# Encoder block on one core: the down projection's block outputs summed in DRAM by adding DMAs, its activation forms shared by both column halves, and 32 instead of 20 tiles of gate and up as block products

## The chip, the cores and the metric

The kernel runs on one core of a Trainium2 chip. The metric is the device time of one execution in microseconds (us), the median of several. The engines are named as in the profile: PE (TensorE, matrix products; PEld is its weight load), DVE (VectorE), ACT (ScalarE), POOL (GpSimd) and SP (SyncE, which here only issues DMAs).

## The reference, cut to what matters

```python
def reference(x, norm_mix, w_in, w_fourier, sgu_norm, w_spatial, b_spatial, w_out,
              norm_ffn, w_gate, w_up, w_down, norm_final):
    ...  # token mixing (Fourier heads and spatial gating) and the output projection, added to x
        h2 = rmsnorm(x, norm_ffn[l])
        x = x + (jax.nn.silu(h2 @ w_gate[l]) * (h2 @ w_up[l])) @ w_down[l]
    return rmsnorm(x, norm_final)
```

There are 512 tokens, the model width is 2048, the width of the feed-forward part 5632, all in float32. Only the feed-forward part (gate, up, down) and its sum into x are touched here.

## The kernel before, in words

Every float32 product is made of three products of rounded halves: an operand is split into `hi` (a cast on ACT, L173) and `lo` (the rest, a subtraction on DVE, L174), and PE computes hi·hi, hi·lo and lo·hi (L85 to L87, L705 to L707, L791 to L793).

The feed-forward part has 44 tiles of 128 features (FT). They are worked in three ways, in this order.

*Direct units.* A `GateUp` item is a quarter of the work of a tile: eight of the sixteen slices of the model width, for gate or for up. It loads 512 KB of weights, splits them, and runs 24 matmuls with 512 moving columns. Two units make gate, two make up. The first 4 tiles are worked so, and the last 20.

*Block products for gate and up.* Tiles 4 to 23 are worked in pairs. Gate (or up) of a pair is a 2x2 block product, done with seven products in place of eight in a Winograd-like scheme (`Matrix`, `Block`). Each of the seven takes 24 matmuls with 256 moving columns; the forms of h2 are prepared once (`Forms`).

*Block products for the down projection* (`Product`). The activations of the first 40 tiles go to a DRAM buffer `ad` and come back as `ac`. For each of ten groups q of four tiles and each half np_ of the output columns, seven products are made, 140 in all. A product takes 12 matmuls with 512 columns. On DVE it needs: `sums` (sums of weight blocks of 128x1024, and of activation blocks of 128x512: the form x), `prep` (the split of the form X, 128x512, and of the weights, 128x1024), and `out`, which adds the product from PSUM into output blocks that stay in SBUF. Before, these are eight blocks `x` of 128x1024 (they start as the x of the residual, read from the DRAM buffer `xd` by `Outputs`) and two common sums `u`; `Fold` adds u to the blocks after the last product. Then come four `Last` items and the tail with the last four tiles, the final norm and the store.

`drive` writes the order of PE, DVE, ACT, POOL and SP by hand. At item k it records the sums of item k+3, the split of item k+2, the loads of items k+4 to k+8, then the matmuls and the `out` of item k. So DVE, which works in order, stands at the `out` of item k until PE has ended it, with items k+1 and k+2 split. The list `items` sets how products are mixed with direct units: `LAG` units come first, and then products are spread evenly over the units that follow. All 512 KB buffers of this part share a pool of 26 slots (`spool`).

Of the kernel before, what the change touches and what calls it, by code (L numbers as in the profile page):

```python
# [10 lines left out]
F32 = mybir.dt.float32  # L11
# [25 lines left out]
FIRST, BLOCKS = 4, 20  # L37
# [3 lines left out]
def encoder_block(ctx, tc, a, out):  # L41
# [21 lines left out]
    def slot(name, dtype=F32, shape=(P, U)):  # L63
        return spool.tile(list(shape), dtype, tag="s", name=name)
# [374 lines left out]
    xd = dram.tile([NT, 2, P, U], F32, name="xd")  # L439
# [170 lines left out]

    GORDER = (1, 6, 2, 7, 5, 4, 3)
# [109 lines left out]

    PRODUCTS = {}

    class Product(Item):
# [19 lines left out]
        def sums(self):  # L744
            i, r = self.i, PRODUCTS[self.q, self.np_]
            A11, A12, A21, A22 = self.blocks()
            add, sub = nc.vector.tensor_add, nc.vector.tensor_sub
            if i == 1:
                add(r[12], r[12], r[22])
            elif i == 6:  # L750
                x = slot(f"x{self.name}", F32, (P, 2, 2, H))
                r["x5"], r["x6"] = x[:, 0], x[:, 1]
                sub(r["x5"], A21, A22)
                sub(r["x6"], r["x5"], A11)
                add(r[11], r[11], r[12])
            elif i == 5:
                add(r[21], r[21], r[11])
                sub(r[11], r[11], r[22])
            elif i == 7:
                sub(r["x5"], A11, A21)  # L760
            elif i == 3:
                add(r["x6"], r["x6"], A12)

        def behind(self, y):
            same = isinstance(y, Product) and (y.q, y.np_) == (self.q, self.np_)
            return same and (y.i, self.i) in ((1, 6), (2, 5), (5, 7))

        def prep(self):
            i, r = self.i, PRODUCTS[self.q, self.np_]
            A11, A12, A21, A22 = self.blocks()  # L770
            x = {1: A11, 2: A12, 4: A22, 5: r.get("x5"), 7: r.get("x5")}.get(i, r.get("x6"))
            self.X = slot(f"X{self.name}", F32R, (P, 2, 2, H))
            split(x, (self.X[:, 0], self.X[:, 1]))
            raw = r[{1: 11, 6: 11, 2: 21, 7: 12, 5: 11, 4: 21, 3: 22}[i]]
            self.split_weights(raw, f"d{self.name}")
# [31 lines left out]
    class Fold(Item):


        def __init__(self, np_):  # L810
            self.np_ = np_

        def out(self):
            for t in range(2):
                for k in (12, 21, 22):
                    d = out_block(k, t, self.np_)
                    nc.vector.tensor_tensor(d, d, usum[self.np_][:, t, :], op=ALU.add if k == 21 else ALU.subtract)
# [75 lines left out]
    items += [Fold(0), Fold(1), Split(1)]  # L893
# [3 lines left out]
    works = [x for x in items if not isinstance(x, (Split, Fold, Forms, Outputs))]  # L897
# [159 lines left out]
```

## Time and profile before

| | |
|---|---|
| time, median of 3 runs | 1861.09 us (1860.4 to 1861.54) |
| profiled execution | 1861.64 us, span 1859.9 us |
| granted TensorE clock, mean | 0.995 of full speed |
| PE, DVE, ACT, POOL busy | 1837.2, 1432.5, 738.7, 84.4 us |
| tiles 4 to 23 as block products | about 574 to 981 us |
| direct units mixed with down products | 981 to 1798 us |

The shares are averages over stages; what limits a stage is read from its own window.

### The profile page before, as it was taken

How to read it: one execution, taken by the hardware profiler on the slowest of the kernel's cores; microseconds unless marked ns; L12 is line 12 of the kernel's file. 1: busy time of each engine (PE TensorE's matmuls, PEld its weight loads, DVE VectorE, ACT ScalarE, POOL GpSimd, SP SyncE). 2: the span in 40 equal slices, each digit the busy share in tenths (PEclk: the TensorE clock that was granted, in tenths of full speed). 3: DMA queues.
4: the chain of work that ended last, by engine and by line, in shares of the span. 5: the costliest groups of instructions: out<-in, count | busy, mean ns of one | idle time of the engine just before them, and what ended most of it. 6: DMA issues, size and time to landing. Idle time of an engine off the chain costs nothing.

```text
span 1859.9 us, 24373 instructions
## 1 busy us (share of the span) xinstructions
PE 1837.2 (99%) x9810; PEld 1592.8 (86%) x9810; DVE 1432.5 (77%) x1805; ACT 738.7 (40%) x950; POOL 84.4 (5%) x82
## 2 busy tenths in 40 slices
PE   9999999999999999999999999999999999999996
PEld 7888888888888999999998888888888888888875
DVE  7554654333578888888887899999899889889987
ACT  6345532222333434444443433334333434334334
POOL 5001110000000000000000000000000000000004
PEclk9999999999999999999999999999999999999998
DMA  7322224442441433433328323333232433323223
GB/s 243 98 76 95 91 80 145 138 136 91 134 172 69 135 127 104 134 115 103 111 72 294 136 91 124 131 141 136 91 136 91 165 118 116 122 102 117 98 79 126
DMA packets 65201, 227.12 MB, mean 122 GB/s; under 512 B 7616, under 2 KB 7744, under 8 KB 65088
## 3 DMA queue, kind: packets, MB, share of 16 engines
q1 hardware_dynamic: 60768, 209.83, 32.8%
q0 software_dynamic: 4320, 15.73, 2.2%
q8 instruction: 77, 1.26, 0.3%
q14 instruction: 36, 0.29, 0.1%
HBM read 206.66 MB, written 18.87 MB: 121 GB/s over the span
## 4 chain that ended last, share of the span: by engine, by line
PE 95%; DVE 2%; ACT 1%; issue 0%; DMA 0%; POOL 0%; SPq 0%; ACTq 0%; DVEq 0%
PE d L793 7%; PE d L792 7%; PE d L791 7%; PE g L86 5%; PE g L87 5%; PE g L85 5%; PE up L86 4%; PE up L87 4%; PE up L85 4%; PE upb L707 4%; PE upb L706 4%; PE upb L705 4%; PE gb L707 4%; PE gb L705 4%; PE gb L706 4%; PE o L87 3%
## 5 line engine op out<-in xcount | busy, mean ns | idle before, releaser
L791 PE MATMUL d<-hi_d,X 128*128 128x512 f32 x560 | 217.8, 389 | 0.0
L792 PE MATMUL d<-lo_d,X 128*128 128x512 f32 x560 | 217.8, 389 | 0.0
L793 PE MATMUL d<-hi_d,X 128*128 128x512 f32 x560 | 217.8, 389 | 0.0
L173 ACT CAST hi_d<-w 128x1024 fp32r<-128x1024 f32 x140 | 147.5, 1053 | 153.9 <-PE d L793 54.5
L174 DVE TENSOR_TENSOR lo_d<-w,hi_d 128x1024 fp32r<-128x1024 f32 x140 | 170.4, 1217 | 5.2 <-ACT hi_d L173 5.2
L85 PE MATMUL up<-h2hi,hi_up 128*128 128x512 f32 x384 | 149.5, 389 | 0.0
L85 PE MATMUL g<-h2hi,hi_g 128*128 128x512 f32 x384 | 149.5, 389 | 0.0
L86 PE MATMUL up<-h2lo,hi_up 128*128 128x512 f32 x384 | 149.4, 389 | 0.0
L86 PE MATMUL g<-h2lo,hi_g 128*128 128x512 f32 x384 | 149.4, 389 | 0.0
L87 PE MATMUL g<-h2hi,lo_g 128*128 128x512 f32 x384 | 149.4, 389 | 0.0
L87 PE MATMUL up<-h2hi,lo_up 128*128 128x512 f32 x384 | 149.4, 389 | 0.0
L802 DVE TENSOR_TENSOR x<-d,x 128x512 f32<-128x512 f32 x200 | 130.4, 682 | 0.0
L792 PEld LDWEIGHTS d<-lo_d,X 128*128 128x128 f32 x560 | 105.1, 188 | 21.8
L791 PEld LDWEIGHTS d<-hi_d,X 128*128 128x128 f32 x560 | 105.1, 188 | 21.8
L793 PEld LDWEIGHTS d<-hi_d,X 128*128 128x128 f32 x560 | 105.1, 188 | 21.7
L80 DVE TENSOR_TENSOR lo_o<-raw_o,hi_o 128x1024 fp32r<-128x1024 f32 x32 | 39.2, 1225 | 102.4 <-ACT hi_o L79 102.4
L173 ACT CAST hi_gb<-w_gb 128x1024 fp32r<-128x1024 f32 x70 | 73.4, 1049 | 92.8 <-DVE w_gb L640 26.6
L173 ACT CAST hi_upb<-w_upb 128x1024 fp32r<-128x1024 f32 x70 | 73.5, 1049 | 84.7 <-PE upb L706 29.2
L174 DVE TENSOR_TENSOR lo_upb<-w_upb,hi_upb 128x1024 fp32r<-128x1024 f32 x70 | 85.4, 1221 | 23.5 <-ACT hi_upb L173 23.5
L174 DVE TENSOR_TENSOR lo_gb<-w_gb,hi_gb 128x1024 fp32r<-128x1024 f32 x70 | 85.5, 1221 | 22.1 <-ACT hi_gb L173 22.1
L173 ACT CAST hi_g<-raw_g 128x1024 fp32r<-128x1024 f32 x48 | 50.3, 1054 | 111.5 <-PE up L86 35.3
L706 PE MATMUL gb<-hf,hi_gb 128*128 128x256 f32 x320 | 90.7, 283 | 0.4 <-DVE hf L174 0.4
(319 smaller groups left out, 4835.3 us busy)
## 6 DMA issues: line engine op xcount, KB each, us to landing
w<-in_w_down SPq DMA_DIRECT2D x80, 512.0 KB, 6.0
raw_g<-in_w_gate SPq DMA_DIRECT2D x48, 512.0 KB, 3.6
raw_up<-in_w_up SPq DMA_DIRECT2D x48, 512.0 KB, 3.5
w_gb<-in_w_gate SPq DMA_DIRECT2D x40, 512.0 KB, 4.2
w_upb<-in_w_up SPq DMA_DIRECT2D x40, 512.0 KB, 4.4
raw_o<-in_w_out SPq DMA_DIRECT2D x32, 512.0 KB, 3.5
ac<-ad SPq DMA_DIRECT2D x20, 512.0 KB, 5.2
raw_v<-in_w_v SPq DMA_DIRECT2D x16, 512.0 KB, 3.5
```

Source lines behind the costliest of these rows:

```text
L85: mm(ps, lhs[0], rhs[0], start=first, stop=False)
L86: mm(ps, lhs[0], rhs[1], start=False, stop=False)
L87: mm(ps, lhs[1], rhs[0], start=False, stop=last)
L173: nc.scalar.copy(dst[0], src)
L174: nc.vector.tensor_sub(dst[1], src, dst[0])
L705: mm(ps, lhs[0], rhs[0], start=first, stop=False, skip_group_check=True)
L706: mm(ps, lhs[0], rhs[1], start=False, stop=False, skip_group_check=True)
L707: mm(ps, lhs[1], rhs[0], start=False, stop=last, skip_group_check=True)
L791: mm(p, X[:, 0, j, l], hi, start=j == 0 and not more, stop=False, skip_group_check=True)
L792: mm(p, X[:, 0, j, l], lo, start=False, stop=False, skip_group_check=True)
L793: mm(p, X[:, 1, j, l], hi, start=False, stop=j == 1, skip_group_check=True)
L802: nc.vector.tensor_add(d, self.ps[t], d)
```

## The change

Gate and up: `BLOCKS` grows from 20 to 32, so tiles 4 to 35 are block products, and 8 tiles (32 units) are left as direct units after them instead of 20 (80 units). Down: the residual is written to a DRAM buffer `cd` in the shape of the eight output blocks. The running sums of a 7-product set now live in two buffers `u` and `w`; the four output blocks of a set are written to a buffer `c` and added to `cd` by a DMA of POOL with `accum_op=add`. `Outputs` reads `cd` back once, after the products; `Fold` is gone. The forms x and their splits X are made for np_ 0 alone and kept for np_ 1. The order of the seven becomes 1, 6, 2, 7, 5, 4, 3. The products are spread over the units 1 to 26 of 32 (`LAG, END = 1, 5`) instead of 3 to 78 of 80.

```diff
-FIRST, BLOCKS = 4, 20
+FIRST, BLOCKS = 4, 32
...
-                nc.gpsimd.dma_start(xd[m, n // 2], x2[m][n // 2])
+                to = cd[n // 2, m // 2, :, :, m % 2, :].rearrange("c p s -> p c s")
+                nc.gpsimd.dma_start(to, x2[m][n // 2].rearrange("p (c s) -> p c s", s=S))
...
-    ORDER = (1, 6, 2, 5, 7, 3, 4)
+    ORDER = (1, 6, 2, 7, 5, 4, 3)
...
-                usum[np_] = slot(f"u{np_}", F32, (P, 2, S))
-                nc.gpsimd.memset(usum[np_], 0.0)
-                for k in (11, 22, 12, 21):
+                for k in (11, 12, 21, 22):
                     t = cs_[k, np_] = slot(f"x{k}_{np_}", F32, (P, 2, S))
+                    nc.sync.dma_start(t, cd[np_, k // 10 - 1, k % 10 - 1])
...
         def sums(self):
+            if self.np_ == 0:
+                A11, A12, A21, A22 = self.blocks()
+                if i == 6:
+                    x = slot(f"x{self.name}", F32, (P, 2, 2, H))
+                    r["x5"], r["x6"] = x[:, 0], x[:, 1]
+                    sub(r["x5"], A21, A22)
+                    sub(r["x6"], r["x5"], A11)
+                elif i == 7:
+                    r["x7"] = slot(f"x{self.name}", F32, (P, 2, H))
+                    sub(r["x7"], A11, A21)
+                elif i == 3:
+                    add(r["x6"], r["x6"], A12)
...
         def prep(self):
+            if self.np_ == 0:
...
+                X = XS[self.q, i] = slot(f"X{self.name}", F32R, (P, 2, 2, H))
+                split(x, (X[:, 0], X[:, 1]))
+            self.X = XS[self.q, i]
...
         def out(self):
-                nc.vector.tensor_add(d, self.ps[t], d)
-                if i == 7:
-                    d = out_block(22, t, np_)
-                    nc.vector.tensor_sub(d, d, self.ps[t])
-    class Fold(Item):
...
+                if i == 1:
+                    nc.scalar.copy(u, ps)
+                elif i == 6:
+                    nc.vector.tensor_add(u, ps, u)
+                elif i == 2:
+                    nc.scalar.copy(c[:, t, :], ps)
+                elif i == 7:
+                    nc.vector.tensor_add(w, ps, u)
+                elif i == 5:
+                    nc.vector.tensor_sub(c[:, t, :], ps, w)
+                elif i == 4:
+                    nc.vector.tensor_add(c[:, t, :], ps, w)
                 else:
+                    nc.vector.tensor_sub(c[:, t, :], ps, u)
+            if to:
+                nc.gpsimd.dma_start(cd[self.np_, to // 10 - 1, to % 10 - 1], c, accum_op=ALU.add)
...
-    LAG = 3
+    LAG, END = 1, 5
...
-        want = min(len(products), len(products) * max(0, n + 1 - LAG) // (len(units) - LAG - 1))
+        want = min(len(products), len(products) * max(0, n + 1 - LAG) // (len(units) - LAG - END))
...
+        if n == len(units) - END + 1:
+            items.append(Outputs())
```

On DVE, in a set of the second column half (np_ 1), from the split of product 2 on. Names read tile, q, np_, product; `raw_g` and `act` belong to direct units. Before:

```order
L174 TENSOR_TENSOR X0_1_2_9294<-ac1_8673,X0_1_2_9294 128x512
L174 TENSOR_TENSOR lo_d0_1_2_9298<-w21_0_1_9080,hi_d0_1_2_9297 128x1024
L757 TENSOR_TENSOR w21_0_1_9080<-w21_0_1_9080,w11_0_1_9053 128x1024
L758 TENSOR_TENSOR w11_0_1_9053<-w11_0_1_9053,w22_0_1_9057 128x1024
L802 TENSOR_TENSOR u1_8850<-d0_1_6_0_9303,u1_8850 128x512
L802 TENSOR_TENSOR u1_8850<-d0_1_6_1_9304,u1_8850 128x512
L174 TENSOR_TENSOR X0_1_5_9319<-x0_1_6_9218,X0_1_5_9319 128x512
L174 TENSOR_TENSOR lo_d0_1_5_9323<-w11_0_1_9053,hi_d0_1_5_9322 128x1024
L760 TENSOR_TENSOR x0_1_6_9218<-ac0_8671 128x512
L174 TENSOR_TENSOR lo_g26_1_9355<-raw_g26_1_9195,hi_g26_1_9354 128x1024
L802 TENSOR_TENSOR x11_1_8852<-d0_1_1_0_9278,x11_1_8852 128x512
L802 TENSOR_TENSOR x11_1_8852<-d0_1_1_1_9279,x11_1_8852 128x512
```

Now, in the same half of another group:

```order
L174 TENSOR_TENSOR lo_d4_1_2_13520<-w21_4_1_13352,hi_d4_1_2_13519 128x1024
L756 TENSOR_TENSOR w21_4_1_13352<-w21_4_1_13352,w11_4_1_13296 128x1024
L554 TENSOR_TENSOR act19_12907<-g39_13377,rstdB_101 128x512
L758 TENSOR_TENSOR w11_4_1_13296<-w11_4_1_13296,w22_4_1_13300 128x1024
L174 TENSOR_TENSOR lo_d4_1_7_13563<-w12_4_1_13298,hi_d4_1_7_13562 128x1024
L566 SCALAR_TENSOR_TENSOR act19_12907<-s39_13558,act19_12907 128x512
L806 TENSOR_TENSOR uw4_1_1_13516<-d4_1_6_0_13569,uw4_1_1_13516 128x512
L806 TENSOR_TENSOR uw4_1_1_13516<-d4_1_6_1_13570,uw4_1_1_13516 128x512
L174 TENSOR_TENSOR lo_d4_1_5_13586<-w11_4_1_13296,hi_d4_1_5_13585 128x1024
L174 TENSOR_TENSOR lo_d4_1_4_13606<-w21_4_1_13352,hi_d4_1_4_13605 128x1024
```

The splits X, the form x and the outputs of products 1 and 2 are gone from DVE in this half. In the first half (np_ 0) the splits and forms stay, as here between the products 3 and 2 of two sets:

```order
L174 TENSOR_TENSOR X4_0_1_13237<-ac8_13091,X4_0_1_13237 128x512
L174 TENSOR_TENSOR lo_d4_0_1_13241<-w11_4_0_13095,hi_d4_0_1_13240 128x1024
L744 TENSOR_TENSOR x4_0_6_13244<-ac8_13091,ac9_13093 128x512
L745 TENSOR_TENSOR x4_0_6_13244<-x4_0_6_13244,ac8_13091 128x512
L754 TENSOR_TENSOR w11_4_0_13095<-w11_4_0_13095,w12_4_0_13097 128x1024
L814 TENSOR_TENSOR c3_1_4_13262<-d3_1_4_0_13248,uw3_1_7_13181 128x512
L814 TENSOR_TENSOR c3_1_4_13262<-d3_1_4_1_13249,uw3_1_7_13181 128x512
L174 TENSOR_TENSOR X4_0_6_13266<-x4_0_6_13244,X4_0_6_13266 128x512
L174 TENSOR_TENSOR lo_d4_0_6_13270<-w11_4_0_13095,hi_d4_0_6_13269 128x1024
L816 TENSOR_TENSOR c3_1_3_13285<-d3_1_5_0_13219,uw3_1_1_13115 128x512
L816 TENSOR_TENSOR c3_1_3_13285<-d3_1_5_1_13220,uw3_1_1_13115 128x512
L174 TENSOR_TENSOR X4_0_2_13289<-ac9_13093,X4_0_2_13289 128x512
```

All of this stands ahead of the split of product 2, without a wait for a direct unit between. On POOL, the whole queue of the down stage before was two memsets and a store of activations per pair of tiles:

```order
L715 MEMSET u0_8836 128x1024
L715 MEMSET u1_8850 128x1024
L524 DMA ad_3618<-act12_8893 128x1024
L524 DMA ad_3618<-act13_9438 128x1024
L524 DMA ad_3618<-act14_10053 128x1024
```

Now it issues the adding DMAs, four per set:

```order
L818 DMA cd_2420<-c0_0_2_11658 128x1024
L818 DMA cd_2420<-c0_0_5_11707 128x1024
L818 DMA cd_2420<-c0_0_4_11763 128x1024
L818 DMA cd_2420<-c0_0_3_11783 128x1024
L818 DMA cd_2420<-c0_1_2_11860 128x1024
```

Six of the eight stores of activations in this stage are gone, and 80 adding DMAs have come.

## Rows read from the trace of the kernel before

**Rows 1.** The page: the span, busy times by engine, and the chain that ended last by engine.

```profile
span 1859.9 us, 24373 instructions
PE 1837.2 (99%) x9810; PEld 1592.8 (86%) x9810; DVE 1432.5 (77%) x1805; ACT 738.7 (40%) x950; POOL 84.4 (5%) x82
...
PE 95%; DVE 2%; ACT 1%; issue 0%; DMA 0%; POOL 0%; SPq 0%; ACTq 0%; DVEq 0%
```

**Rows 2.** What PE waited for in the whole run: waiting line, waited-for line, us in total, times, longest (the four that lie in the feed-forward part).

```profile
PE l L85 <- DVE x L843: 2.0, 1, 2.0
...
PE gb L705 <- ACT t_gb L671: 0.8, 1, 0.8
PE gb L707 <- DVE lo_gb L174: 0.5, 1, 0.5
PE gb L706 <- DVE hf L174: 0.4, 1, 0.4
```

**Rows 3.** Busy time by stretch: stretch, its us, then busy us (instructions) of PE, PEld, DVE, ACT, POOL, granted clock, mean busy share of the 16 DMA engines, GB/s. The first is the block products of gate and up, the third nearly the whole stage with the down products, the last its end.

```profile
581.00:981.00 400.00, 398.90 (x3309) 398.70 (x3310) 340.92 (x356) 167.41 (x190) 4.78 (x9) 1.00 0.34 113
981.00:990.00 9.00, 9.00 (x43) 7.51 (x42) 5.16 (x5) 1.05 (x1) 2.39 (x3) 1.00 0.98 360
990.00:1790.00 800.00, 800.00 (x3531) 662.65 (x3530) 720.48 (x915) 315.58 (x380) 4.25 (x8) 1.00 0.35 125
1790.00:1824.00 34.00, 31.98 (x135) 26.00 (x134) 30.06 (x43) 8.80 (x10) 0.00 (x0) 0.95 0.38 123
```

**Rows 4.** The tile view of the gate block product: the first evacuation of each of the ten gate matrices, with first and last start.

```profile
L671 ACT COPY t_gb<-gb x10: 365/373/375, 581.2 to 944.1; 128x256 f32<-128x256 f32 x10
```

**Rows 5.** DVE in order of time in the down stage: start, busy us, instruction.

```profile
1031.80 0.68 DVE L174 TENSOR_TENSOR X<-ac,X 128x512 fp32r<-128x512 f32 x1
1032.40 1.22 DVE L174 TENSOR_TENSOR lo_d<-w,hi_d 128x1024 fp32r<-128x1024 f32 x1
1033.54 1.22 DVE L749 TENSOR_TENSOR w<-w,w 128x1024 f32<-128x1024 f32 x1
1034.68 1.22 DVE L174 TENSOR_TENSOR lo_up<-raw_up,hi_up 128x1024 fp32r<-128x1024 f32 x1
...
1038.74 0.68 DVE L753 TENSOR_TENSOR x<-ac,ac 128x512 f32<-128x512 f32 x1
1039.46 0.69 DVE L754 TENSOR_TENSOR x<-x,ac 128x512 f32<-128x512 f32 x1
1040.07 1.22 DVE L755 TENSOR_TENSOR w<-w,w 128x1024 f32<-128x1024 f32 x1
...
1049.68 1.22 DVE L757 TENSOR_TENSOR w<-w,w 128x1024 f32<-128x1024 f32 x1
1050.94 1.23 DVE L758 TENSOR_TENSOR w<-w,w 128x1024 f32<-128x1024 f32 x1
```

**Rows 6.** The tile view of the down products' PSUM tile d: matmuls of one of the three kinds, and the DVE instructions that read d (duration ns min/median/max, first and last start).

```profile
L793 PE MATMUL d<-hi_d,X x560: 389/389/389, 1003.6 to 1791.7; 128*128 128x512 f32 x187
L802 DVE TENSOR_TENSOR x<-d,x x200: 673/681/692, 1017.2 to 1792.3; 128x512 f32<-128x512 f32 x100
L802 DVE TENSOR_TENSOR u<-d,u x80: 677/681/691, 1006.4 to 1769.1; 128x512 f32<-128x512 f32 x80
L805 DVE TENSOR_TENSOR x<-x,d x40: 671/676/679, 1030.0 to 1784.6; 128x512 f32<-128x512 f32 x40
```

**Rows 7.** What DVE waited for between 990 and 1798 us: us in total, times, longest.

```profile
DVE act L551 <- PE g L87: 25.3, 19, 3.0
DVE s L556 <- PE up L87: 20.4, 15, 3.1
...
DVE w L749 <- DMA w<-in_w_down: 3.2, 1, 3.2
```

**Rows 8.** DVE in order of time at the end of the down stage.

```profile
1798.94 7.30 DVE L817 TENSOR_TENSOR x<-x,u 128x512 f32<-128x512 f32 x12
...
1809.64 2.47 DVE L843 TENSOR_TENSOR x<-l,x 128x512 f32<-128x512 f32 x4
```

**Rows 9.** PE in order of time at the same place; in brackets the idle time before it and what ended it.

```profile
1808.05 0.39 PE L87 MATMUL l<-hi_dk,al 128*128 128x512 f32 x1
1810.46 0.47 PE L85 MATMUL l<-hi_dk,al 128*128 128x512 f32 x1 [2.02 <-DVE x L843]
...
1811.52 0.63 PE L86 MATMUL l<-lo_dk,al 128*128 128x512 f32 x1
...
1814.50 0.53 PE L87 MATMUL l<-hi_dk,al 128*128 128x512 f32 x1
1814.87 0.40 PE L85 MATMUL l<-hi_dk,al 128*128 128x512 f32 x1
```

**Rows 10.** DMA issues by line: count, KB each, median us from issue to landing.

```profile
w<-in_w_down SPq DMA_DIRECT2D x80, 512.0 KB, 6.0
...
ad<-act POOLq DMA_DIRECT2D x10, 512.0 KB, 3.0
ad<-o_gb POOLq DMA_DIRECT2D x10, 512.0 KB, 5.0
```

**Rows 11.** Groups of ACT instructions by shape: busy us, mean ns of one, idle before.

```profile
L252 ACT COPY ey<-E 128x258 f32<-128x258 f32 x8 | 3.0, 379 | 0.0
...
L173 ACT CAST X<-ac 128x512 fp32r<-128x512 f32 x58 | 35.7, 615 | 0.0
```

More of the change, by code (lines that the diff above doesn't have):

```diff
@@ L437, in x2c @@
         return x2[m][n // 2][:, (n % 2) * S : (n % 2 + 1) * S]
-    xd = dram.tile([NT, 2, P, U], F32, name="xd")
+    cd = dram.tile([2, 2, 2, P, 2, S], F32, name="cd")
     xss = const.tile([P, NT, 4], F32, name="xss")
@@ L713, in out @@
             for np_ in range(2):
-                usum[np_] = slot(f"u{np_}", F32, (P, 2, S))
-                nc.gpsimd.memset(usum[np_], 0.0)
-                for k in (11, 22, 12, 21):
+                for k in (11, 12, 21, 22):
                     t = cs_[k, np_] = slot(f"x{k}_{np_}", F32, (P, 2, S))
-                    n = 2 * np_ + k % 10 - 1
-                    for i in range(2):
-                        nc.sync.dma_start(t[:, i, :], xd[2 * (k // 10 - 1) + i, np_, :, (n % 2) * S : (n % 2 + 1) * S])
+                    nc.sync.dma_start(t, cd[np_, k // 10 - 1, k % 10 - 1])
     PRODUCTS = {}
+    XS = {}
     class Product(Item):
@@ L750, in sums @@
             elif i == 6:
[L751 to L754, printed above, removed]
                 add(r[11], r[11], r[12])
+            elif i == 7:
+                add(r[21], r[21], r[11])
             elif i == 5:
-                add(r[21], r[21], r[11])
                 sub(r[11], r[11], r[22])
[L759 to L762, printed above, removed]
         def behind(self, y):
             same = isinstance(y, Product) and (y.q, y.np_) == (self.q, self.np_)
-            return same and (y.i, self.i) in ((1, 6), (2, 5), (5, 7))
+            return same and (y.i, self.i) in ((1, 6), (2, 7))
         def prep(self):
             i, r = self.i, PRODUCTS[self.q, self.np_]
[L770 to L773, printed above, removed]
+            if self.np_ == 0:
+                A11, A12, A21, A22 = self.blocks()
+                x = {1: A11, 2: A12, 4: A22, 5: r.get("x5"), 7: r.get("x7")}.get(i, r.get("x6"))
+                X = XS[self.q, i] = slot(f"X{self.name}", F32R, (P, 2, 2, H))
+                split(x, (X[:, 0], X[:, 1]))
+            self.X = XS[self.q, i]
             raw = r[{1: 11, 6: 11, 2: 21, 7: 12, 5: 11, 4: 21, 3: 22}[i]]
@@ L795, in out @@
         def out(self):
-            i, np_ = self.i, self.np_
-            for t in range(2):
-                if i in (1, 6):
-                    d = usum[np_][:, t, :]
-                else:
-                    d = out_block({2: 11, 5: 22, 3: 12, 7: 21, 4: 21}[i], t, np_)
-                nc.vector.tensor_add(d, self.ps[t], d)
-                if i == 7:
-                    d = out_block(22, t, np_)
-                    nc.vector.tensor_sub(d, d, self.ps[t])
-    class Fold(Item):
[L810 to L817, printed above, removed]
+            i, r = self.i, PRODUCTS[self.q, self.np_]
+            if i in (1, 7):
+                r["u" if i == 1 else "w"] = slot(f"uw{self.name}", F32, (P, 2, S))
+            to = {2: 11, 5: 22, 4: 21, 3: 12}.get(i)
+            if to:
+                c = slot(f"c{self.name}", F32, (P, 2, S))
+            for t in range(2):
+                ps = self.ps[t]
+                u, w = (r[k][:, t, :] if k in r else None for k in ("u", "w"))
+                if i == 1:
[4 more added lines that the diff above has]
+                    nc.scalar.copy(c[:, t, :], ps)
+                elif i == 7:
+                    nc.vector.tensor_add(w, ps, u)
[3 more added lines that the diff above has]
+                    nc.vector.tensor_add(c[:, t, :], ps, w)
+                else:
+                    nc.vector.tensor_sub(c[:, t, :], ps, u)
+            if to:
+                nc.gpsimd.dma_start(cd[self.np_, to // 10 - 1, to % 10 - 1], c, accum_op=ALU.add)
     fr = const.tile([P, NT], F32, name="fr")
@@ L878, in encoder_block @@
             m = Matrix(p, up)
-            items += [Block(m, i) for i in GORDER]
+            items += [Block(m, i) for i in ORDER]
     units = units[4 * (FIRST + BLOCKS) :]
@@ L882, in encoder_block @@
     done = 0
-    LAG = 3
+    LAG, END = 1, 5
     for n, x in enumerate(units):
         items.append(GateUp(*x))
-        if n == 0:
-            items.append(Outputs())
         if n == len(units) - 8:
             items.append(Split(0))
-        want = min(len(products), len(products) * max(0, n + 1 - LAG) // (len(units) - LAG - 1))
+        want = min(len(products), len(products) * max(0, n + 1 - LAG) // (len(units) - LAG - END))
         items += products[done:want]
         done = want
-    items += [Fold(0), Fold(1), Split(1)]
+        if n == len(units) - END + 1:
+            items.append(Outputs())
+    items.append(Split(1))
     items += [Last(n) for n in range(4)]
     tails = [Tail(n) for n in range(4)]
-    works = [x for x in items if not isinstance(x, (Split, Fold, Forms, Outputs))]
+    works = [x for x in items if not isinstance(x, (Split, Forms, Outputs))]
     todo = [x for x in works if isinstance(x, RawUnit)]
```

5 lines of the change are left out of this document (removed).

## Prediction, before the run

> **What bounds the kernel now.** I read the page's busy times and chain first: PE is busy for 1837 of 1859.9 us and 95% of the chain is PE [rows 1], so time goes down only where PE gets fewer or shorter matmuls, or stops waiting. Second, what PE waited for: in the feed-forward part 0.8, 0.5 and 0.4 us where the block products begin, and 2.0 us at the end, on DVE [rows 2]. Third, the stretches, because the change touches three of them: between 581 and 981 us and between 990 and 1790 us PE has no gap, at the full granted clock; DVE is busy for 341 of 400 us in the first and for 720 of 800 us in the second; the DMA engines stand at 35% [rows 3]. So DVE, at 90%, is the next bound of the down stage, and what it waits for there is PE, at the ends of direct units: 25.3 and 20.4 us [rows 7].
>
> **Gate and up: 12 tiles more as block products.** In the down stage PE runs 3531 matmuls of 512 columns in 800 us, 0.2266 us each [rows 3]. A pair of tiles as direct units is 8 units of 24 matmuls, 8 x 5.44 = 43.5 us. A pair as block products is read from the first evacuation of the ten gate matrices: 581.2 to 944.1 us are nine pairs, 40.32 us each [rows 4]. That is 3.2 us a pair, and six pairs give **-19.1 us**, if DVE keeps up as it did there (85% busy [rows 3]); the added pairs have the same instructions.
>
> A rule speaks for more. The Trainium skill ("TensorE: Matmul & The Clock Gate", section "Wait — 56ns, not 53.3ns?") gives columns over 2.4 GHz plus about 2.5 ns a matmul: by it, an estimate, 192 x 0.2158 = 41.4 us against 336 x 0.1092 = 36.7 us, or 28 us for six pairs and a time about 9 us lower. The trace disagrees at both shapes, 0.2266 us here and 40.32 / 336 = 0.120 us there [rows 3, 4].
>
> **The end of the stage.** The twelve `Fold` instructions take DVE 7.3 us just after the last unit [rows 8]. The first `Last` evacuation comes so late that PE, which needs its bank, waits 2.0 us; after that the granted clock falls to the lower of its levels, 1.2 of 2.4 GHz, and from 1811.52 to 1814.50 us a matmul starts every 0.43 us in place of 0.23 [rows 9]. Idle 2.0, restart 0.2, seven slow steps and two half-slow ones 1.6: **-3.8 us**. What is late next there is nothing of DVE: it keeps 4.7 us of work (two splits, four additions) to the 5.4 us of PE in each `Last`. The read-back of `cd`, 8 x 512 KB, is issued after unit 28 and needed 3 units and one `Last` later, 21.8 us; at 360 GB/s [rows 3] it takes 12 us.
>
> **DVE in the down stage.** From the starts of successive instructions: a 128x1024 instruction costs 1.14 us, 1.26 where it follows one on the same tile; a 128x512 one 0.60, or 0.72 [rows 5]. Before, a set of seven products costs: weight splits 7 x 1.14 = 8.0, form splits 7 x 0.60 = 4.2, weight sums 4.8, forms 2.5, and 16 evacuations (320 over 20 sets [rows 6]) 9.6; together 29.1 us. A direct unit costs 1.14 for its split and a quarter of 2.52 for the four operations of a tile, 1.8 us. Twenty sets and 80 units are 724 us, which agrees with the 720 measured [rows 3].
>
> Now an np_ 0 set has ten evacuations: 8.0 + 4.2 + 4.8 + 2.5 + 6.0 = 25.5 us. An np_ 1 set has no forms either: 18.8 us. But between two units there are now 140 / 26 = 5.4 products, not 1.8, so a set has only 1.3 units beside it. PE needs 7 x 2.72 + 1.3 x 5.44 = 26.1 us a set; DVE needs 27.8 us in np_ 0 and 21.1 us in np_ 1. Over both DVE has room, but it can't save it: it works at most two items ahead, since the third needs the `out` of an item that PE hasn't ended. So each np_ 0 set is 1.7 us too long for PE, 17 us over ten sets.
>
> The bounds: below, a set begins with DVE two products ahead: after the `out` (1.2) and the next split (1.7) 2.5 of 5.4 us are left, which could cover the 1.7 each time: 0. Above, a walk through an np_ 0 set without a unit in it: DVE stands at the `out` of product 5 of the set before while PE still has 4 and 3. Work of DVE up to the split of 6 ends at 8.3 us where PE needs it at 8.2, up to that of 2 at 11.3 (PE 11.1), of 7 at 16.0 (PE 14.0), of 5 at 19.0 (PE 18.7); product 3 adds to the bank of 5 and so needs its `out`, at 26.6 (PE 24.4). That is 4.8 us of waits. A unit inside the set gives 3.6 back, but less when it comes while DVE is ahead anyway; so 0 to some 30 us over ten sets. I take 1.5 us a set, near the 1.7 of the balance: **+15 us**. The np_ 1 sets wait for nothing.
>
> **The start of the stage.** Products now follow two units, not four, so PE needs the first at 981.4 + 10.9 = 992.3 us. Before, DVE waited for its weights until 988.85, 3.2 us [rows 7]; a sum and two splits from there end at about 991.8, those of product 6 some 1 us late: **+1 us**, 0 to 4.
>
> **ACT.** It gets four evacuations a set: 0.38 us for 256 columns, 0.62 us for a cast of 512 [rows 11], so 80 of about 0.6, and loses 70 form casts of 0.62. At 316 of 800 us busy [rows 3] it hides both; a product 2 that must wait for the copy of 1 has product 6 (2.7 us) between.
>
> **POOL and DMA.** Eighty adding DMAs of 512 KB are new; no row shows one. Plain stores of POOL land in 3.0 to 5.0 us [rows 10], and one is issued every 6.6 us, so at that price nothing waits for them but slots. From above: the stage's loads (80 weights, 20 activations, 32 units) are 69 MB in 555 us, 125 GB/s or 35% of the engines as before [rows 3]; 42 MB to be added cost 21% for each plain transfer that an addition is worth. I take two and no time; weights are loaded five items (16 us) ahead and landed in 6.0 [rows 10].
>
> **Sum**, against the profiled execution's 1861.6 us: -19.1 - 3.8 + 15 + 1 = 1854.7; the median of the runs shown is 0.5 lower, so **1854 us**.
>
> **Rivals.**
>
> *A, the cover holds.* DVE's waits stay under 9 us, because units fall where the first half of a set needs them. For it: the 2.5 us lead. Against it: the walk, where product 7 alone is 2.0 us late. With 0 to 9 us: 1839 to 1848, say 1844.
>
> *B, DVE takes the whole gain.* Sets without an early unit dominate (3 us each), or a wait near 2 us halves the clock after it, as at 1810 us, for 1.6 us more each time [rows 9]. Against it: waits of 0.8, 0.5 and 0.4 us in a row left the clock full between 574 and 581 us [rows 2]. With 22 to 32 us of waits 1861 to 1871, say 1864.
>
> *C, slower: the adding DMAs become the bound.* One mechanism in the DMA engines of the down stage: if an addition costs k plain transfers, the share is 35% + 21% x k. It decides from k = 3.1, where the engines are full; at k = 4 the stage takes 119% of 555 us, 105 us more, 1945 us. Well before that, loads that land in 6 us would land late. For it: each addition must read what it changes before it writes it. Against it: 65% of the engines are free.
>
> By the Trainium skill ("Collectives: The Full Stack", section "The bandwidth ceiling: the fold count and why AG ≠ RS ≠ AR") an addition in the DMA path is slower only because it reads two sources, about twice a copy. By that rule k is 2, the share 77%, and C doesn't happen; no run here shows it yet.
>
> That the outputs don't leave DVE after all is no rival: the order shows it.
>
> **How the numbers follow.** The forecast, with 9 to 20 us of waits (1848 to 1859), has a chance of 0.45; A 0.17; B 0.26; C or late loads 0.12. 0.2%, 3.7 us, is about what a measurement can tell from no change: faster is below 1857.4, slower above 1864.8. Faster: 0.43 of the forecast and all of A, 0.60. Same: 0.02 and a bit more than half of B, 0.17. Slower: the rest of B and C, 0.23. The forecast's own range is 1848 to 1859; for 8 in 10 it runs from 1842 (A's lower part out) to 1870 (most of B in, C out).
>
> **What would show it.** Block products at 40.3 us a pair, sixteen of them; no wait of PE at the first `Last` and no slow matmuls there; DVE at about 500 us in the down stage; PE's waits on DVE (splits `lo_d`, X) in the first half of np_ 0 sets, at products 7 and 3, 1 to 2 us each, none in np_ 1 sets. It is wrong if PE waits for DMA or slots, if the waits don't lie in np_ 0 sets, or if the granted clock falls in the stage.

## The result, and the profile after

The changed kernel takes 1849.61 us (median of 4 runs, 1848.85 to 1850.23) against 1860.74 us before in the same comparison: ratio 0.9941, 95% interval 0.9924 to 0.9958. The gain is small, 0.6%, but clear of the noise. The profiled execution took 1850.23 us, span 1848.5 us. The forecast was 1854 us.

The page, as in [rows 1]: the span, the busy times, the chain.

```profile
span 1848.5 us, 26416 instructions
PE 1820.0 (98%) x10674; PEld 1614.0 (87%) x10674; DVE 1407.4 (76%) x1683; ACT 785.0 (42%) x1014; POOL 152.5 (8%) x160
...
PE 89%; DVE 7%; issue 2%; ACT 1%; DMA 0%; POOL 0%; SPq 0%; ACTq 0%; DVEq 0%
```

PE lost 17 us of busy time, and the chain now runs 7% of the span through DVE, where it was 2%. The windows (columns as in [rows 3]) say where:

```profile
581.00:981.00 400.00, 398.36 (x3315) 397.96 (x3316) 343.10 (x359) 167.55 (x191) 4.81 (x9) 1.00 0.36 120
985.00:1222.00 237.00, 237.00 (x1977) 237.00 (x1976) 201.74 (x211) 99.23 (x113) 2.67 (x5) 1.00 0.36 120
1232.00:1765.00 533.00, 526.09 (x2298) 429.56 (x2297) 485.97 (x579) 255.51 (x323) 69.92 (x82) 1.00 0.78 195
1765.00:1813.00 48.00, 48.00 (x213) 39.74 (x213) 27.50 (x35) 12.00 (x13) 0.00 (x0) 1.00 0.67 231
```

The block products (first two lines) keep PE busy, the end of the stage (last line) has no gap and no slow clock any more. The loss is in the third line, the down products: PE has gaps of 7 us there and DVE is busy for 486 of 533 us. What PE waited for in the down stage:

```profile
PE d L790 <- DVE lo_d L174: 4.0, 8, 1.0
PE d L789 <- DVE c L812: 2.4, 2, 1.6
PE up L87 <- DVE lo_up L174: 0.2, 1, 0.2
PE g L87 <- DVE lo_g L174: 0.2, 1, 0.2
```

These 6.8 us are not all. A matmul of 512 columns counts as busy for 0.39 us, but the next may start after 0.2267, so the first 0.16 us of any delay are booked as busy. I therefore measure the stage from the start of its first direct unit to the start of the first `Last`. These are two lines of PE in order of time of the kernel before, and then the same two of the changed one:

```profile
981.37 0.40 PE L85 MATMUL g<-h2hi,hi_g 128*128 128x512 f32 x1
...
1797.40 0.39 PE L85 MATMUL l<-hi_dk,al 128*128 128x512 f32 x1
```

```profile
1222.62 0.40 PE L85 MATMUL g<-h2hi,hi_g 128*128 128x512 f32 x1
...
1789.99 0.39 PE L85 MATMUL l<-hi_dk,al 128*128 128x512 f32 x1
```

Before, 80 units and 140 products, 3600 matmuls, took 816.03 us, 0.2267 us each; this is the pitch of PE when nothing holds it up. Now it is 32 units and 140 products, 2448 matmuls: 554.9 us at that pitch, 567.4 measured. The difference, 12.5 us, I call the **late time** of the stage. (The texts of expectation below say 11.7 us; that is what the single delays over 0.05 us add up to.) The block products ran 241.25 us longer for the 48 units that they replace (261.1 us): -19.9 us. The four `Last` took 25.6 us before and 21.8 now: -3.9 us. Together these are -11.3 us, where the spans of the two profiled executions differ by 11.4.

### The profile page after: what moved, and what is told of

Same layout as the page of the kernel before. It is cut to its first block, busy times and chain, and to the rows that moved or that the text cites. A ratio compares the mean times of both kernels' runs of the same rounds, so it can differ in the third digit from the quotient of the medians.

```text
span 1848.5 us, 26416 instructions
## 1 busy us (share of the span) xinstructions
PE 1820.0 (98%) x10674; PEld 1614.0 (87%) x10674; DVE 1407.4 (76%) x1683; ACT 785.0 (42%) x1014; POOL 152.5 (8%) x160
## 3 DMA queue, kind: packets, MB, share of 16 engines
q1 hardware_dynamic: 59616, 209.83, 33.7%
## 4 chain that ended last, share of the span: by engine, by line
PE 89%; DVE 7%; issue 2%; ACT 1%; DMA 0%; POOL 0%; SPq 0%; ACTq 0%; DVEq 0%
PE upb L702 6%; PE upb L700 6%; PE upb L701 6%; PE gb L702 6%; PE gb L701 6%; PE gb L700 6%; PE d L790 5%; PE d L791 5%; PE d L789 5%; PE o L87 3%; PE o L85 3%; PE o L86 3%; PE g L87 2%; PE g L86 2%; PE g L85 2%; PE up L87 2%
## 5 line engine op out<-in xcount | busy, mean ns | idle before, releaser
L173 ACT CAST hi_gb<-w_gb 128x1024 fp32r<-128x1024 f32 x112 | 117.5, 1049 | 150.0 <-PE upb L701 43.7
L174 DVE TENSOR_TENSOR lo_upb<-w_upb,hi_upb 128x1024 fp32r<-128x1024 f32 x112 | 136.8, 1221 | 37.3 <-ACT hi_upb L173 37.3
L174 DVE TENSOR_TENSOR lo_gb<-w_gb,hi_gb 128x1024 fp32r<-128x1024 f32 x112 | 136.7, 1221 | 34.4 <-ACT hi_gb L173 34.4
L702 PE MATMUL gb<-hf,lo_gb 128*128 128x256 f32 x512 | 145.0, 283 | 0.5 <-DVE lo_gb L174 0.5
L701 PE MATMUL gb<-hf,hi_gb 128*128 128x256 f32 x512 | 145.0, 283 | 0.4 <-DVE hf L174 0.4
L700 PE MATMUL gb<-hf,hi_gb 128*128 128x256 f32 x512 | 144.9, 283 | 0.0
L700 PE MATMUL upb<-hf,hi_upb 128*128 128x256 f32 x512 | 144.9, 283 | 0.0
L701 PE MATMUL upb<-hf,hi_upb 128*128 128x256 f32 x512 | 144.9, 283 | 0.0
L702 PE MATMUL upb<-hf,lo_upb 128*128 128x256 f32 x512 | 144.9, 283 | 0.0
L80 DVE TENSOR_TENSOR lo_o<-raw_o,hi_o 128x1024 fp32r<-128x1024 f32 x32 | 39.2, 1226 | 102.4 <-ACT hi_o L79 102.4
L700 PE MATMUL gb<-h2hi,hi_gb 128*128 128x256 f32 x384 | 108.8, 283 | 0.8 <-ACT t_gb L666 0.8
L702 PE MATMUL gb<-h2hi,lo_gb 128*128 128x256 f32 x384 | 108.8, 283 | 0.5 <-DVE lo_gb L174 0.5
L700 PE MATMUL upb<-h2hi,hi_upb 128*128 128x256 f32 x384 | 108.7, 283 | 0.0
```

Source lines behind the costliest of these rows:

```text
L80: nc.vector.tensor_sub(lo[:, c], raw[:, c], hi[:, c])
L173: nc.scalar.copy(dst[0], src)
L174: nc.vector.tensor_sub(dst[1], src, dst[0])
L700: mm(ps, lhs[0], rhs[0], start=first, stop=False, skip_group_check=True)
L701: mm(ps, lhs[0], rhs[1], start=False, stop=False, skip_group_check=True)
L702: mm(ps, lhs[1], rhs[0], start=False, stop=last, skip_group_check=True)
```

## The experiments

There are three theories for the 12.5 us. *DVE theory*: sets of np_0 give DVE more work than PE has. *ACT theory*: the copies of products 1 and 2 stand in ACT's queue ahead of the casts that DVE and PE wait for. What DVE waited for in the stage speaks for it; the first line was 5.2 us in the kernel before.

```profile
DVE lo_d L174 <- ACT hi_d L173: 28.1, 28, 3.6
DVE s L559 <- PE up L87: 11.4, 5, 3.1
DVE act L554 <- PE g L87: 7.3, 5, 3.4
```

*DMA theory*: the adding DMAs take the DMA engines and the slots that loads need. The share of 0.78 speaks for it, and so do two groups of the waits of SP, which waits for `cd<-c` before it can load:

```profile
SPq L730 <- DMA cd<-c: 79.5, 12, 21.0
...
SPq L726 <- DMA cd<-c: 70.9, 4, 20.4
```

The late times given below are all worked out as above, with the number of matmuls of each kernel.

### The two parts, each alone

```diff
-FIRST, BLOCKS = 4, 32
+FIRST, BLOCKS = 4, 20
```

> The down projection's part of the change alone: 20 tiles as block products as before, 80 direct units. DVE theory (PE's loss in the down stage, 11.7 us of late starts in the changed kernel, comes from sets of np_0 in which DVE has more work than PE): here a set has (80 - 6) / 20 = 3.7 units beside it, PE needs 19.0 + 3.7 x 5.44 = 39.2 us and DVE 25.5 + 3.7 x 1.8 = 32.2 us, so the sets lose nothing; the time is before's less the 3.8 us of the end, plus 0 to 1 us at the start: 1857 to 1859 us. ACT theory (the casts are late because ACT does the copies of products 1 and 2 first, and these wait for PE): the same copies stand ahead of the same casts, DVE waits for hi_d about 28 us as in the changed kernel, and PE loses part of the 11 us: 1860 to 1868 us. DMA theory (the adding DMAs delay the loads): the 80 additions are spread over 816 us instead of 555, the loss is small: 1857 to 1860 us.

The run took 1856.84 us (ratio 0.9982, 0.9973 to 0.9992), with a late time of 0.0 and `Last` at 21.8 us in place of 25.6. DVE is busy for 597 of 815 us of the stage, where it was 729. So the new down part by itself gives only what the end gives; the 132 us of DVE's work that it saves shorten nothing while DVE has cover. The copies stand ahead of the casts here as well, and PE doesn't wait. This is a weak point against the ACT theory, since with so many units DVE has time to make good what it loses to a late cast.

In the kernel before, the other way round:

```diff
-FIRST, BLOCKS = 4, 20
+FIRST, BLOCKS = 4, 32
```

> The block products' part alone: 32 tiles, with the down products as before. DVE theory: a set costs DVE 29.1 us and has 28 / 20 = 1.4 units beside it, 2.5 us more, 31.6 in all; PE needs 19.0 + 7.6 = 26.7 us. DVE is the bound of all twenty sets, 4.9 us each, 98 us: 1861.6 - 19.1 + 98 = 1940 us (1925 to 1950). If DVE isn't what bounds these sets: 1842.5 us, the gain of the pairs alone.

The run took 1958.07 us (ratio 1.0527, 1.0506 to 1.0548), above the expected range. The window of the stage (columns as in [rows 3]):

```profile
1224.00:1894.00 670.00, 593.71 (x2445) 465.83 (x2444) 640.34 (x826) 256.87 (x323) 3.45 (x5) 0.97 0.33 112
```

DVE is busy for 96% of it, as expected, and the late time is 116 us. The balance of DVE and PE gave 98. Where the other 18 us come from is open. The granted clock, 0.97 in the mean, stood at its lower level for some 40 us, in which PE does the work of 20; but DVE, the bound here, waited for PE for 2.4 us only, and for 20 us for casts of ACT and 4 us for a load, which the balance left out as well. The block products can't be added without the new down part, and the new down part brings little without them: the change is one of DVE's work traded for PE's.

### ACT: the copies on DVE

```diff
-                    nc.scalar.copy(u, ps)
+                    nc.vector.tensor_copy(u, ps)
...
-                    nc.scalar.copy(c[:, t, :], ps)
+                    nc.vector.tensor_copy(c[:, t, :], ps)
```

> The changed kernel with the copies of products 1 and 2 out of PSUM on DVE instead of ACT. DVE theory: each set costs DVE four instructions of 0.60 us more, 2.4 us; a set of np_0 goes from 27.8 to 30.2 us against PE's 26.1 and loses about 3.5 us instead of 1.1, a set of np_1 (23.5 us) still waits for nothing: 1870 to 1878 us. ACT theory: the casts no longer wait behind copies, DVE's waits for hi_d fall from 28.1 us to under 10, and PE's loss falls with them: 1840 to 1848 us. DMA theory: 1850 us.

The run took 1871.31 us (ratio 1.0060, 1.0044 to 1.0077), with a late time of 33.7. DVE's waits for the casts fell as the ACT theory wanted, and the time rose all the same. DVE's first line of waits, and then PE's, in the stage of this kernel:

```profile
DVE lo_d L174 <- ACT hi_d L173: 11.1, 18, 1.6
```

```profile
PE d L789 <- DVE uw L804: 10.7, 8, 2.6
PE d L790 <- DVE lo_d L174: 5.4, 10, 1.1
PE d L789 <- DVE c L812: 5.1, 5, 2.6
```

The ACT theory falls: 17 us of DVE's idle time went and PE lost 21 us more. Idle time of DVE in front of a cast lay mostly where DVE was ahead: in the changed kernel about 27 of the 34 us that DVE waits for ACT while products run begin while PE is in an np_1 set, and PE lost nothing there. PE's first group of waits is new: product 2 adds to the bank of product 1 and now waits for DVE to have copied that out. So the 21 us are the price of DVE's added work and of this new wait together, and 3.8 us of the late time lie in np_1 sets, where none was expected.

### DMA: plain stores

```diff
-                nc.gpsimd.dma_start(cd[self.np_, to // 10 - 1, to % 10 - 1], c, accum_op=ALU.add)
+                nc.gpsimd.dma_start(cd[self.np_, to // 10 - 1, to % 10 - 1], c)
```

> The changed kernel with plain stores in place of the adding DMAs: the sum over the ten groups is left out, each block is overwritten. DMA theory: a store moves each byte without reading what is there, the share of the DMA engines falls from 0.78 to about 0.58 in the stage, loads land earlier, and PE's loss of 11.7 us goes: 1839 to 1845 us. DVE theory and ACT theory: nothing that DVE or ACT waits for changes: 1848 to 1851 us, with 10 to 12 us of late starts on PE at the same products of np_0.

The run took 1849.40 us (ratio 0.9943, 0.9929 to 0.9958), with a late time of 12.5, the same as with additions, at the same products. The DMA engines have less to do, and so has POOL. Below are the window of this kernel, then what its page says of the 80 DMAs (at the end the median us from issue to landing), then what the page of the changed kernel says of them:

```profile
1232.00:1765.00 533.00, 526.11 (x2298) 429.52 (x2297) 485.94 (x579) 255.51 (x323) 43.69 (x82) 1.00 0.55 196
```

```profile
cd<-c POOLq DMA_DIRECT2D x80, 512.0 KB, 3.6
```

```profile
cd<-c POOLq DMA_DIRECT2D x80, 512.0 KB, 7.2
```

The DMA theory falls: 0.23 of the DMA engines' share went and no time with it. SP's two groups of waits for `cd<-c` became shorter, 59.0 and 60.1 us, without any effect on PE. The run also prices an addition. By an estimate that takes the loads at 0.35 of the engines as in the stage before [rows 3], plain stores take 0.20 and adding ones 0.43: an addition costs k = 2.15 plain transfers. The Trainium skill's rule for collectives ("Collectives: The Full Stack", section "The bandwidth ceiling: the fold count and why AG ≠ RS ≠ AR") of two sources read, so about twice a copy, agrees with the 2.15.

### DVE's balance: where the units stand, and how many there are

All direct units into the np_0 sets, by weighting the products of np_1 with 0 when they are spread over the units:

```diff
+    W = (1.0, 0.0)
+    full = sum(W[x.np_] for x in products)
...
-        want = min(len(products), len(products) * max(0, n + 1 - LAG) // (len(units) - LAG - END))
+        part = min(1.0, max(0, n + 1 - LAG) / (len(units) - LAG - END))
+        want = done
+        while want < len(products) and sum(W[x.np_] for x in products[: want + 1]) <= part * full + 1e-6:
+            want += 1
```

> The changed kernel with all 26 direct units that are mixed with products put into the np_0 sets (2.6 each) and none into the np_1 sets. DVE theory: a set of np_0 then takes PE 19.0 + 2.6 x 5.44 = 33.1 us and DVE 25.5 + 2.6 x 1.8 = 30.2 us, a set of np_1 PE 19.0 and DVE 18.8 us; both have room, so most of the 11.7 us of late starts goes: 1839 to 1842 us, under 3 us of late starts. ACT theory: the same copies stand ahead of the same casts in both halves; PE loses about as much as before: 1847 to 1851 us.

The run took 1843.02 us (ratio 0.9907, 0.9893 to 0.9920), with a late time of 5.5 in place of 12.5. This is a little above what the DVE theory gave for the time and for the late time, and the time is far below the 1847 to 1851 us of the ACT theory. Not an instruction more or less is in this kernel, only the order differs, and it is faster than the kernel before and the changed one.

The same with 34 tiles as block products:

```diff
-FIRST, BLOCKS = 4, 32
+FIRST, BLOCKS = 4, 34
```

> The same with 34 tiles as block products, so 24 direct units, 18 of them among the products. DVE theory: the added pair gives 3.2 us; a set of np_0 has 1.8 units, PE 28.8 us and DVE 28.7, np_1 as in the run before: no room left, but no loss in the balance: 1836 to 1840 us. ACT theory: 1844 to 1848 us.

The run took 1845.46 us (ratio 0.9921, 0.9907 to 0.9935), a miss: the pair's gain went into 10.8 us of late time. The time lies in the range of the ACT theory (1844 to 1848 us), so this run alone doesn't part the two. All but 0.6 us of the delays that can be assigned lie in np_0 sets, where DVE's and PE's sums are equal (28.7 and 28.8 us). Such a set has no loss on paper; that it loses because DVE's work comes in lumps is argued, not shown.

The changed kernel with 28 tiles, the units spread evenly:

```diff
-FIRST, BLOCKS = 4, 32
+FIRST, BLOCKS = 4, 28
```

> The changed kernel with 28 tiles as block products instead of 32, units spread evenly: 42 units over twenty sets, 2.1 each. DVE theory: a set of np_0 costs DVE 25.5 + 3.8 = 29.3 us against PE's 30.5, so the late starts fall from 11.7 to 0 to 3 us, while two pairs less cost 6.4 us: 1845 to 1848 us, somewhat faster than the changed kernel although it has fewer block products. If the loss isn't DVE's balance and stays at 11 us: 1856 us.

The run took 1848.12 us (ratio 0.9935, 0.9923 to 0.9948), at the upper end of what was expected, with a late time of 3.4. It has two block pairs less, 6.4 us of PE's work more, and is no slower than the changed kernel, because 9 us of late time went. What DVE waits for its casts rose to 53.8 us in this run, while PE waited less: once more against the ACT theory.

### The forms made twice

```diff
-            if self.np_ == 0:
+            if True:
```

(in `sums` and in `prep`)

> The changed kernel with the forms of the activations and their splits made again for the second half, as they were before: 6.7 us more of DVE in each np_1 set, 27.8 us against PE's 26.1 in all twenty sets. DVE theory: no set has room any more in which DVE could get ahead again, so each loses 1.7 us or more, 34 us in place of 11.7: 1868 to 1880 us, with about half of the late starts in np_1. If sharing were worth nothing: 1850 us.

The run took 1876.83 us (ratio 1.0088, 1.0074 to 1.0102), with a late time of 38.1. Of the delays over 0.15 us that I could assign, 16.3 us lie in np_0 and 13.9 in np_1, where the changed kernel has none. So the sharing of the forms is worth 26 us of late time here, and without it the kernel is slower than before the change.

### The forms on POOL

```diff
-                    sub(r["x5"], A21, A22)
-                    sub(r["x6"], r["x5"], A11)
+                    nc.gpsimd.tensor_sub(r["x5"], A21, A22)
+                    nc.gpsimd.tensor_sub(r["x6"], r["x5"], A11)
```

(and the same for the other two)

> The changed kernel with the four subtractions and additions that make the forms of the activations on POOL instead of DVE, nothing else. DVE theory: a set of np_0 loses 2.5 us of DVE's work, 25.3 us against PE's 26.1, so the 11.7 us of late starts fall to 0 to 4: 1839 to 1843 us. Rival (POOL becomes the wait): POOL takes 1.3 us for such an instruction where DVE takes 0.6, and in its queue they stand behind adding DMAs that wait for DVE; the splits of products 6, 7 and 3 then wait for POOL, and the late starts stay at 10 us or more: 1848 to 1853 us.

The run took 1880.92 us (ratio 1.0110, 1.0096 to 1.0124), with a late time of 43.7, far above what either theory gave. PE waits in np_0 sets for `lo_d`, 20.1 us, as if DVE had got more work and not less. It has. These are POOL and then DVE in order of time in this kernel:

```profile
1282.09 1.61 POOL L744 TENSOR_TENSOR x<-ac,ac 128x512 f32<-128x512 f32 x1
1283.78 2.16 POOL L745 TENSOR_TENSOR x<-x,ac 128x512 f32<-128x512 f32 x1
```

```profile
1281.15 0.68 DVE L174 TENSOR_TENSOR X<-ac,X 128x512 fp32r<-128x512 f32 x1
1281.75 3.04 DVE L174 TENSOR_TENSOR lo_d<-w,hi_d 128x1024 fp32r<-128x1024 f32 x1
1284.82 2.20 DVE L754 TENSOR_TENSOR w<-w,w 128x1024 f32<-128x1024 f32 x1
1286.94 1.28 DVE L814 TENSOR_TENSOR c<-d,uw 128x512 f32<-128x512 f32 x2
```

Beside a subtraction on POOL, DVE's split takes 3.04 us and its sum 2.20, where both take 1.22 alone. DVE is busy for 529.3 us in the stage, 26 us more than in the changed kernel (502.9), although 40 instructions of 0.65 us have left it: some 52 us of stretching, 5.2 us a set. A set of np_0 thus costs DVE about 30.5 us, as in the run with the copies on DVE, and PE loses 10 us more than there, some of it at the lower clock. DVE's instructions that read one operand from PSUM are not stretched:

```profile
1400.65 1.27 DVE L816 TENSOR_TENSOR c<-d,uw 128x512 f32<-128x512 f32 x2
```

These two ran beside a POOL subtraction from 1399.72 to 1401.88 us and took the usual 1.27 together. The Trainium skill ("SBUF — State Buffer", section "Who interferes with whom") says so: a DVE instruction with two inputs in SBUF contends with a POOL instruction that reads SBUF, one with a single SBUF input, outside the modes that use both ports, does not. The trace agrees: the first kind took 3.04 and 2.20 us in place of 1.22, the second its usual 1.27.

Two variants of it, with the units spread by weights as above, and 34 tiles in the first:

```diff
+    W = (1.0, 0.4)
```

> The forms on POOL, 34 tiles as block products, and the 18 units spread so that a product of np_1 counts 0.4 of one of np_0: 1.3 units a set in np_0, 0.5 in np_1. DVE theory: np_0 takes DVE 23.0 + 2.3 = 25.3 us against PE's 26.0, np_1 19.7 against 21.8, so there is room in both halves, and the pair gives 3.2 us: 1836 to 1840 us. If POOL becomes the wait: 1845 us or more.

> The same with 32 tiles, 1.9 units a set in np_0 and 0.7 in np_1. DVE theory: np_0 takes DVE 26.4 us against PE's 29.1, np_1 20.1 against 22.8; late starts under 2 us: 1839 to 1841 us. If POOL becomes the wait: 1845 us or more.

The two runs took 1888.02 us (ratio 1.0148, 1.0132 to 1.0163) and 1867.54 us (1.0040, 1.0027 to 1.0052), with late times of 53.4 and 30.2. Both miss for the reason of the first; that more units beside np_0 still help (43.7 to 30.2) fits the DVE theory, with DVE's work as it really was.

### The end alone: the kernel before without Fold

```diff
-    items += [Fold(0), Fold(1), Split(1)]
+    items += [Split(1)]
```

> The kernel before without its twelve fold instructions at the end of the stage (it leaves out adding the common sums u to the blocks), nothing else. If the 7.3 us of Fold on DVE cause PE's wait of 2.0 us at the first Last and the slow matmuls behind it: 3.8 us less, 1856 to 1858 us, no wait there and no matmul at the slow pitch. If the first Last evacuation is late for another reason (its splits, its weights): 1860 us, the wait stays.

The run took 1857.34 us (ratio 0.9981, 0.9972 to 0.9990). `Last` takes 21.8 us in place of 25.6, and PE's wait of 2.0 us [rows 2] is gone. `Fold` was the cause.

### What the runs say together

The table has PE's and DVE's us for a set of np_0, by the prices of the prediction and the expectations (where POOL makes the forms, with the 5.2 us of stretching from above), beside the late time of the stage:

| kernel | PE | DVE | late, us |
|---|---|---|---|
| 20 tiles, new down part | 39.2 | 32.2 | 0.0 |
| 28 tiles | 30.5 | 29.3 | 3.4 |
| 32 tiles, units in np_0 | 33.1 | 30.2 | 5.5 |
| 34 tiles, units in np_0 | 28.8 | 28.7 | 10.8 |
| changed kernel | 26.1 | 27.8 | 12.5 |
| changed, plain stores | 26.1 | 27.8 | 12.5 |
| 32 tiles, forms on POOL, weighted | 29.1 | 31.6 (stretched) | 30.2 |
| changed, copies on DVE | 26.1 | 30.2 | 33.7 |
| changed, forms twice (both halves) | 26.1 | 27.8 | 38.1 |
| changed, forms on POOL | 26.1 | 30.5 (stretched) | 43.7 |
| 34 tiles, forms on POOL, weighted | 26.0 | 30.5 (stretched) | 53.4 |
| kernel before, 32 tiles (both halves) | 26.7 | 31.6 | 116 |

The late time grows where DVE's margin shrinks, though not evenly. The third line stands out of order: it has more margin in np_0 than the second, but none in np_1 (18.8 against 19.0 us). Its two longest waits, 0.85 us each, are at product 6, the second of an np_0 set. I read from that that DVE enters np_0 without a lead there; no run tested it.

## Why the prediction was right

The forecast was 1854 us with its own range 1848 to 1859; measured were 1849.6, 1.6 us above the upper end of rival A (1848). The cause that it named, DVE in the sets of np_0, is what the runs show, for the greater part of the late time. That its size came so near is partly luck: the bounds were 0 and 30 us, and 15 was chosen between them. The sizes, step by step:

- *Six pairs, -19.1 us*: -19.9, or 40.2 us a pair; 0.7 us of the -19.9 comes of the granted clock, which fell near 582 us in the profile before and not in the one after (see rivals A and B below). The first evacuation of the sixteen gate matrices, to be compared with [rows 4], gives fifteen pairs in 604.2 us, 40.28 each:

```profile
L666 ACT COPY t_gb<-gb x16: 364/373/373, 581.2 to 1185.4; 128x256 f32<-128x256 f32 x16
```

  The Trainium skill's rule of 2.5 ns a matmul ("TensorE: Matmul & The Clock Gate", section "Wait — 56ns, not 53.3ns?") would have given 28 us, an estimate; the trace after disagrees with it as the one before did, 40.28 us a pair against 36.7.
- *The end, -3.8 us*: -3.9, and the run without Fold shows its cause. DVE now reaches the first additions of `Last` in time, which it did not in [rows 8]:

```profile
1794.39 1.22 DVE L174 TENSOR_TENSOR dl_lo<-raw_dl,dl_hi 128x1024 fp32r<-128x1024 f32 x1
1795.53 2.48 DVE L844 TENSOR_TENSOR x<-l,x 128x512 f32<-128x512 f32 x4
```

- *DVE in the down stage, +15 us*: it measured 12.5, the start included. (The 724 us of DVE's work that it set out from are those of the whole stage, to be held against 729 measured there and not against the 720 of [rows 3], which leave out its ends.) Every delay over 0.15 us lies in np_0, none in np_1, as predicted. The places were predicted too narrowly: not products 7 and 3 alone, 1 to 2 us each, but 6, 7, 5 and 3, and units in between, 0.2 to 1.8 us. The walk had DVE enter each set at the `out` of product 5; it often enters with more lead, so some sets lose nothing (set 5) and others 1.8 (set 9). One such place, DVE and then PE in order of time:

```profile
1568.39 1.22 DVE L174 TENSOR_TENSOR lo_d<-w,hi_d 128x1024 fp32r<-128x1024 f32 x1
1569.53 1.29 DVE L810 TENSOR_TENSOR uw<-d,uw 128x512 f32<-128x512 f32 x2
1570.72 0.69 DVE L174 TENSOR_TENSOR X<-x,X 128x512 fp32r<-128x512 f32 x1
1571.32 1.22 DVE L174 TENSOR_TENSOR lo_d<-w,hi_d 128x1024 fp32r<-128x1024 f32 x1
1572.46 1.29 DVE L812 TENSOR_TENSOR c<-d,uw 128x512 f32<-128x512 f32 x2
```

```profile
1572.10 0.40 PE L791 MATMUL d<-hi_d,X 128*128 128x512 f32 x1
1573.30 0.47 PE L789 MATMUL d<-hi_d,X 128*128 128x512 f32 x1 [0.79 <-DVE c L812]
```

  DVE runs without a gap here, and product 3 of PE must wait for the `out` of product 5 (L812), which frees the bank it adds to: the mechanism of the walk. But DVE had stood still a few us before. These are ACT and then DVE in order of time:

```profile
1563.31 0.63 ACT L555 ACTIVATE s<-act 128x512 f32<-128x512 f32 x1 [4.23 <-DVE act L554]
1563.85 0.60 ACT L173 CAST X<-x 128x512 fp32r<-128x512 f32 x1
```

```profile
1564.49 0.69 DVE L174 TENSOR_TENSOR X<-x,X 128x512 fp32r<-128x512 f32 x1 [1.21 <-ACT X L173]
1565.44 1.22 DVE L174 TENSOR_TENSOR lo_d<-w,hi_d 128x1024 fp32r<-128x1024 f32 x1 [0.26 <-ACT hi_d L173]
```

  ACT's `s` of a direct unit waits for DVE's `act`, and the cast that DVE needs next stands behind it. DVE loses 1.5 us so in set 0, 1.5 in set 6 and 0.9 in set 9, and 4.5 of the 12.5 us of late time follow in these sets. Up to 3.8 us are thus a hand-over between DVE and ACT and not DVE's work, and neither the prediction nor the three theories had it; no run parts the two. The 3.4 us left in the run with 28 tiles stand behind two such waits of 1.5 us.
- *The start, +1 us*: nothing. The first down product starts 10.9 us after the stage, as PE's two units need.
- *ACT hides its copies at nothing*: right for the time, though DVE waits 28 us for casts. The run with the copies on DVE shows that it costs 21 us to have them there instead.
- *Adding DMAs, two plain transfers and no time*: k = 2.15, a share of 0.78 (predicted 0.77), and no time, as the plain stores show. Rival C needed k = 3.1.
- *Rivals A and B* had the same mechanism with 0 to 9 and 22 to 32 us. The granted clock stayed full in the stage, with waits of up to 1.6 us. But the argument against B, that the waits of 0.4, 0.8 and 0.5 us left the clock full [rows 2], was a misreading. They stand at 580.3, 581.6 and 582.6 us, and in that same trace PE then ran at the lower level until 586 us:

```profile
582.60 0.58 PE L707 MATMUL gb<-h2hi,lo_gb 128*128 128x256 f32 x1 [0.49 <-DVE lo_gb L174]
582.98 0.41 PE L705 MATMUL gb<-h2hi,hi_gb 128*128 128x256 f32 x1
583.19 0.41 PE L706 MATMUL gb<-h2lo,hi_gb 128*128 128x256 f32 x1
583.40 0.41 PE L707 MATMUL gb<-h2hi,lo_gb 128*128 128x256 f32 x1
```

  A matmul of 256 columns starts every 0.21 us there and every 0.12 after 586 us; the granted clock from 583 to 585 us is 0.50. The changed kernel has the same three waits and kept the full clock, so that the clock stayed full in the down stage too may be luck. It costs little there: the block products of 20 tiles took 407.1 us in the profile before and 406.4 in the run without Fold, where the clock didn't fall. B's price for the clock shows in the kernel with the copies on DVE:

```profile
1627.92 0.47 PE L789 MATMUL d<-hi_d,X 128*128 128x512 f32 x1 [2.57 <-DVE uw L804]
...
1629.03 0.63 PE L789 MATMUL d<-hi_d,X 128*128 128x512 f32 x1
1629.45 0.63 PE L790 MATMUL d<-lo_d,X 128*128 128x512 f32 x1
1629.88 0.63 PE L791 MATMUL d<-hi_d,X 128*128 128x512 f32 x1
```

  After 2.57 us of idle PE a matmul of 512 columns starts every 0.43 us, as in [rows 9], at the lower of the two levels, 1.2 GHz.

## What to carry to other kernels

When a change trades work of one engine for another's, add up both engines' work by the smallest stretch over which the second can't get ahead (here a set, since DVE works two items ahead), not over the stage: DVE had 47 us to spare in the stage, and PE still started 12 us late. Spread the lighter items to the stretches where the loaded engine has too much; moving direct units into np_0 sets gave 6.6 us with no instruction changed. And measure PE's losses by the starts of its matmuls, since recorded waits showed 6.8 of 12.5 us.

## What the runs showed of the hardware that was not expected

- POOL arithmetic on SBUF operands isn't free beside DVE: each of 40 subtractions or additions of 128x512 on POOL cost DVE some 1.3 us (52 us over 40) and saved it 0.65. POOL, idle 92% of the time in the changed kernel, took over 26 us of work and the kernel became 31 us slower. POOL's DMA issues, 0.86 us each, stretched nothing: the splits `lo_d` beside one took 1.22 us like the others.
- POOL itself took 1.3 to 3.2 us there, 1.6 in the median, for what is 1.3 us at the kernel's end.
- An adding DMA of 512 KB lands in 7.2 us where the plain one takes 3.6, beside the same loads (medians). In the other kernels with additions the median is 5.4 to 6.7 us.
- After waits of PE of 0.4, 0.8 and 0.5 us in a row the granted clock fell in some executions and not in others (582 us, above).
